# A streaming-encoder layer on one core: row factors of the first block from a natural read, the second block's rows and squares ahead, its accumulators in two own banks

## The chip, the cores and the metric

The kernel runs on one core of one Trainium2 chip. The metric is the device time of one execution in microseconds (us). The kernel before takes 1491.39 us, the median of three runs (1490.81 to 1494.24).

## The reference

One layer over 2048 rows of 1024 channels in float32. `rmsnorm` divides each row by the root of its mean square; this row factor and its place are what the change is about.

```python
def reference(x, p, mix_norm_g, w_in, ...):
    h = x
    for i in range(DEPTH):                      # DEPTH = 1
        hn = rmsnorm(h, mix_norm_g[i])
        proj = hn @ w_in[i]                     # (2048, 3072)
        u, g_ssm, q, k, v, g_attn = jnp.split(proj, SPLITS, axis=-1)
        y_ssm = s5_branch(u, ...)               # diagonal complex state space, GELU, GLU
        y_ssm = y_ssm * jax.nn.silu(g_ssm)
        y_att = stick_breaking_branch(q, k, v, ...) * jax.nn.silu(g_attn)
        h = h + jnp.concatenate([y_ssm, y_att], axis=-1) @ w_out[i]
        ple_gate = jax.nn.sigmoid(rmsnorm(h, ple_norm_g[i]) @ w_ple_gate[i])
        h = h + ple_gate * (p[i] @ w_ple_proj[i])
    return h
```

## The kernel before

The rows are cut into eight blocks of 256 (T0 to T7), each of two halves a and b of 128 rows. Every product of float32 operands is made of three matmuls (`mm3`, L536): each operand is split into a high half (a copy on ScalarE, ACT) and a low half (a subtraction on VectorE, DVE), and high x high, high x low and low x high are added in PSUM.

The first stage, `phase_u` (L546), makes the input of the state-space branch, `ps_u`, in 96 matmuls of 256 columns for each block: four column tiles (`ct`) times eight slices of channels (`c`) times three. T0 comes from a second copy of its rows that the host has turned (channels on partitions); `load_plain` (L552) loads it in pieces between the eight weight tiles and splits both at once, without the row factor. The factor is brought in afterwards: `norms` (L573) squares the turned rows on ACT, in place (L575), adds the eight slices in three steps on GpSimd (POOL, L577), sums over partitions by a matmul with ones (L579), takes the power -1/2 on POOL (L581), puts the factor on a diagonal on DVE (L583) and spreads it by a second matmul (L585) into a `row` tile on ACT (L586). T0's four `ps_u` are then multiplied by `row` on DVE (L633).

T1 to T7 go through `load_x` (L588): the rows are loaded as they lie (L593), squared and summed on ACT (L596), the factor `rs_x` is made by a scaling on DVE (L72) and a power on POOL (L507), the rows are scaled on ACT (L598), turned by 16 transposes of 64 columns on TensorE (PE, L526) into the banks z0 and z1, split from there (`xt<-ps_x`: high halves on ACT L513, low halves on DVE L65), and stored to `hn` (L602) for later stages. Their `ps_u` are copied out on ACT (L635).

Beside this, DVE runs `ssm_chain` (L176) and then `ssm_pack`: the powers and tables of the state-space branch, several hundred small rows on the tiles `ex_`, `sc_`, `pr_`, `pwr`, `pwi`, `cm` and `tabs`. They have no other engine in between.

After `phase_u` come the state-space batches (`ssm_batch`) with the gate products (`ps_sg`) between them, then attention, and the output.

The order on each engine is not that of the code. A planner (`arrange`, L1554) takes all instructions, with what they need of each other, computes a start for each from costs of its own in six turns (`best_order`, L1521; `list_schedule`, L1446), and fixes the order of each engine's instructions by it. Within an engine the instructions run in that order, and one that waits holds up all behind it. Three hints go in: `e.first` (these come ahead of all else), `e.mark(n)` (a place) and `e.later(n)` (DMAs in it are not planned ahead of mark n). All loads of x and all stores of `hn` are on SP's queue, in one order.

[...] `e.bank(name, tags)` takes the next of the tags in turn; before, the accumulators of T0 and of T1 share the banks w0, w1, o and acc, one column tile in each, and T1 can't write them until T0's are multiplied out.

Of the kernel before, what the change touches and what calls it, by code (L numbers as in the profile page):

```python
# [8 lines left out]
F32 = mybir.dt.float32  # L9
F32R = mybir.dt.float32r  # L10
BF16 = mybir.dt.bfloat16
I32 = mybir.dt.int32
AF = mybir.ActivationFunctionType
ALU = mybir.AluOpType
# [4 lines left out]
P = 128  # L19
SEQ = 2048  # L20
DM = 1024
# [17 lines left out]
EPS = 1e-6  # L39
# [24 lines left out]
def vt(nc, out, a, b, op):  # L64
    nc.vector.tensor_tensor(out, a, b, op=op)  # L65


def vs(nc, out, a, s1, op0, s2=None, op1=None):
    if op1 is None:
        nc.vector.tensor_scalar(out, a, s1, None, op0=op0)  # L70
    else:
        nc.vector.tensor_scalar(out, a, s1, s2, op0=op0, op1=op1)  # L72
# [400 lines left out]
def load_w(e, blocks, width, scale, tag="w", pool=None, bufs=None, at=0, act=True, spare=None):  # L473

    nc = e.nc
    out = []
    for c, src in enumerate(blocks, at):
        t = (pool or e.wpool).tile([P, 2, width], F32R, tag=tag, name=f"w_{tag}", **({"bufs": bufs} if bufs else {}))
        hi, lo = t[:, 0], t[:, 1]
        if spare is None or c < STB + STA:  # L480
            raw = e.stage[c % len(e.stage)].tile([P, 512], F32, tag="wst", name="wst")[:, :width]
        else:
            raw = spare.tile([P, L, NCH // 2], F32, tag="uq", name="wst", bufs=4).rearrange("p j c -> p (j c)")[:, :width]
        if c == MARK0 and spare is not None:
            e.mark(0)
        e.wdma(raw.rearrange("p (k c) -> p k c", k=src.shape[1]) if len(src.shape) == 3 and src.shape[0] == P else raw, src)
        if scale is None:
            split(e, hi, lo, raw)
        else:
            if act:  # L490
                nc.scalar.activation(hi, raw, AF.Copy, scale=scale[:, c:c + 1])  # L491
            else:
                vs(nc, hi, raw, scale[:, c:c + 1], ALU.mult)
            stt(nc, lo, raw, scale[:, c:c + 1], hi.bitcast(F32), ALU.mult, ALU.subtract)
        out.append(t)
    return out


def row_blocks(src, n, c0):
    return [src[c * P:(c + 1) * P, c0:c0 + 512] for c in range(n)]  # L500


def rms_rstd(e, pool, ss, n, width, tag):
    nc = e.nc
    r = pool.tile([P, n], F32, tag=f"rs_{tag}", name=f"rs_{tag}")
    vs(nc, r, ss, 1.0 / width, ALU.mult, EPS, ALU.add)
    nc.gpsimd.tensor_tensor(r, r, e.mhalf[:, :n], op=ALU.pow)  # L507
    return r


def split(e, hi, lo, src):

    e.nc.scalar.activation(hi, src, AF.Copy)  # L513
    vt(e.nc, lo, src, hi.bitcast(F32), ALU.subtract)
# [14 lines left out]
def turned(e, name, tags, views):  # L529
    ps, views = turned_into(e, name, tags, views)  # L530
    with e.abreast():
        transposes(e, ps, views)
    return [p[:, :64 * len(views)].rearrange("p (k t) -> p k t", t=64) for p in ps]


def mm3(e, out, ws, xs, first, last):  # L536

    wh, wl = ws
    xh, xl = xs
    mm = e.nc.tensor.matmul  # L540
    mm(out, wh, xh, start=first, stop=False)  # L541
    mm(out, wh, xl, start=False, stop=False)  # L542
    mm(out, wl, xh, start=False, stop=last)  # L543


def phase_u(e, pool, xp, chain):  # L546

    nc = e.nc

    plain = []  # L550

    def load_plain(T):  # L552
        xt = xp.tile([P, 2, 2, NC8, P], F32R, tag="xg", name="xt", bufs=2)
        w = []
        for hf in range(2):
            plain.append(pool.tile([P, NC8, P], F32, tag="x", name="x", bufs=XB))
        for c in range(0, NC8, 2):
            cs = slice(c, c + 2)
            for hf in range(2):
                x = plain[2 * T + hf]  # L560
                nc.sync.dma_start(x[:, cs], e.xt[2 * T + hf, :, cs])
                split(e, xt[:, hf, 0, cs], xt[:, hf, 1, cs], x[:, cs])
            if T == 0:
                w += load_w(e, row_blocks(e.w_in[0], NC8, 0)[cs], 512, e.gmix, act=ACT0, spare=pool, at=c)
        for hf in range(2):
            with e.later(1):
                nc.sync.dma_start(e.hn_d[2 * T + hf], xt[:, hf].rearrange("p s c t -> p (s c t)").bitcast(F32))
        return xt, w

    ones = pool.tile([P, P], F32, tag="ones", name="ones")  # L570
    nc.gpsimd.memset(ones, 1.0)

    def norms(i):  # L573
        x, r = plain[i], e.rs[i]
        nc.scalar.activation(x, x, AF.Square)  # L575
        for n in (4, 2, 1):
            nc.gpsimd.tensor_tensor(x[:, :n], x[:, :n], x[:, n:2 * n], op=ALU.add)  # L577
        ps = e.bank("ps_row", "tr", "ssm")
        nc.tensor.matmul(ps[:, :1], x[:, 0], ones[:, :1], start=True, stop=True)  # L579
        vs(nc, r, ps[:, :1], 1.0 / DM, ALU.mult, EPS, ALU.add)  # L580
        nc.gpsimd.tensor_tensor(r, r, e.mhalf[:, :1], op=ALU.pow)  # L581
        d = pool.tile([P, P], F32, tag="dg", name="dg", bufs=1)
        vs(nc, d, e.ident, r, ALU.mult)  # L583
        ps = e.bank("ps_row", "tr", "ssm")
        nc.tensor.matmul(ps[:, :P], ones, d, start=True, stop=True)  # L585
        nc.scalar.activation(e.row[i // 2][:, i % 2 * P:i % 2 * P + P], ps[:, :P], AF.Copy)  # L586

    def load_x(T):  # L588
        xt = xp.tile([P, 2, 2, NC8, P], F32R, tag="xg", name="xt", bufs=2)
        for hf in range(2):  # L590
            t0 = (2 * T + hf) * P
            x = pool.tile([P, DM], F32, tag="x", name="x", bufs=XB)
            nc.sync.dma_start(x, e.x[0, t0:t0 + P, :])  # L593
            jk = pool.tile([P, DM], BF16, tag="jk", name="jk", bufs=1)
            ss = pool.tile([P, 1], F32, tag="ss", name="ss", bufs=2)
            nc.scalar.activation(jk, x, AF.Square, accum_out=ss)  # L596
            rs = rms_rstd(e, pool, ss, 1, DM, "x")
            nc.scalar.activation(x, x, AF.Copy, scale=rs)  # L598
            for h, ps in enumerate(turned(e, "ps_x", ("z0", "z1"), [x[:, c * P:(c + 1) * P] for c in range(NC8)])):
                d = slice(64 * h, 64 * h + 64)  # L600
                split(e, xt[:, hf, 0, :, d], xt[:, hf, 1, :, d], ps)
            nc.sync.dma_start(e.hn_d[2 * T + hf], xt[:, hf].rearrange("p s c t -> p (s c t)").bitcast(F32))  # L602
        return xt

    xts = {}
    with e.first():
        xts[0], w = load_plain(0)
        norms(0)
        norms(1)
        with e.later(0):  # L610
            xts[1] = load_x(1)
    prep = chain()
    for T in range(NT // 2):
        if 2 <= T + 1 < NT // 2:
            xts[T + 1] = load_x(T + 1)
        xt = xts.pop(T - 2, None)
        xt = xts[T]
        if T % 4 == 0:
            uq = [pool.tile([P, L, NCH // 2], F32, tag="uq", name="uq", bufs=4) for ct in range(4)]
        ps = [e.bank("ps_u", "w0", "w1", "o", "acc", *(("z0", "z1") if T < 1 else ()))[:, :256] for _ in range(4)]  # L620
        if T == 2:
            e.mark(T)
        for ct, c in [(ct, c) for c in range(NC8) for ct in range(4)] if T == 0 else [(ct, c) for ct in range(4) for c in range(NC8)]:
            if T == 0 and ct == 0 and c == MARK1:
                e.mark(1)
            cs = slice(ct * P, (ct + 1) * P)
            mm3(e, ps[ct], (w[c][:, 0, cs], w[c][:, 1, cs]), (xt[:, :, 0, c], xt[:, :, 1, c]), c == 0, c == NC8 - 1)
        n = NCH // 8
        for ct in range(4):
            k0 = (T % 4) * n  # L630
            o, out = ps[ct].rearrange("p (c j) -> p j c", j=L), uq[ct][:, :, k0:k0 + n]
            if T < 1:
                vt(nc, out, o, e.row[T].rearrange("p (c j) -> p j c", j=L), ALU.mult)  # L633
            else:
                nc.scalar.activation(out, o, AF.Copy)  # L635
            if T % 4 == 3:
                c0 = (T // 4) * (NCH // 2)
                nc.gpsimd.dma_start(e.u_d[ct][:, :, c0:c0 + NCH // 2].rearrange("j p c -> p j c"), uq[ct])
    return prep, xts
# [405 lines left out]
def hybrid_block_kernel(ctx: ExitStack, tc: tile.TileContext, x, xt, small, p, w_in, ssm_w_glu, w_out, w_ple_gate,  # L1045
# [115 lines left out]
    up = pool(early, "pu")  # L1161
    e.stage += [pool(early, "stage1", STA)] * STA
    prep, xts = phase_u(e, up, gx, lambda: ssm_chain(e, keep, sm))
    with e.later():
        late_consts()
# [448 lines left out]
```

## Time and profile before

| | |
|---|---|
| median of three runs | 1491.39 us (1490.81 to 1494.24) |
| the profiled execution | 1490.92 us |
| its span, first to last instruction | 1489.2 us |
| mean granted TensorE clock | 0.995 |
| PE, DVE, ACT, POOL busy | 97%, 68%, 55%, 32% of the span |

The profile shows that one execution. Its rows give start and duration in us, the engine, the line, the operation, what it writes and reads, the shapes, how many instructions are merged (x2), and in brackets how long the engine stood idle before and what it waited for. Where rows follow each other without a break, the start of the next one says more than the duration, since rows overlap in the pipeline. The tables of stretches give for each stretch its length, the busy time and count of PE, PEld (weight loads), DVE, ACT and POOL, the granted clock, the share of the DMA engines and GB/s.

### The profile page before, as it was taken

The page shows a single profiled execution, that of the slowest core. Times are in us where ns is not written, and L with a number is a line of the kernel's source. Part 1 is how long each engine was busy: PE and PEld are TensorE (multiplying, and loading weights), DVE is VectorE, ACT ScalarE, POOL GpSimd, SP SyncE. Part 2 cuts the span into 40 slices and gives each one's busy share as a digit, 9 for nine tenths or more (in the row PEclk, how much of TensorE's full clock was granted, in tenths as well). Part 3 has the DMA queues.
Part 4 walks back from the last instruction along what each step waited for, and adds up shares of the span by engine and source line. Part 5 has one row for each costly group of instructions (what it writes and reads, how often), then busy time and mean ns, then how long its engine had stood idle before and what let it go on. Part 6 is the DMA issues. An engine that isn't in the chain of part 4 may idle for free.

```text
span 1489.2 us, 33570 instructions
## 1 busy us (share of the span) xinstructions
PE 1444.9 (97%) x13068; PEld 1220.6 (82%) x13068; DVE 1012.0 (68%) x1814; ACT 812.1 (55%) x1764; POOL 469.2 (32%) x512
## 2 busy tenths in 40 slices
PE   5999999999999999999999999999999999999998
PEld 5999989988888888887788877787777888777776
DVE  8943877976567876777766766657777557744544
ACT  5654545565456765566655655566654436533333
POOL 3221354412221111211122114544234555434332
PEclk9999999999999999999999999999999999999999
DMA  8876746645332523334333445766477546423221
GB/s 292 296 267 231 227 135 206 194 152 169 126 131 99 180 99 101 126 120 141 97 125 126 125 131 183 234 223 187 131 243 243 170 156 196 151 76 107 72 67 60
DMA packets 178909, 238.21 MB, mean 160 GB/s; under 512 B 65744, under 2 KB 121024, under 8 KB 167616
## 3 DMA queue, kind: packets, MB, share of 16 engines
q1 hardware_dynamic: 176368, 227.49, 47.2%
q0 software_dynamic: 2384, 8.59, 2.0%
q8 instruction: 103, 1.69, 0.5%
q14 instruction: 54, 0.44, 0.1%
HBM read 166.94 MB, written 64.90 MB: 156 GB/s over the span
## 4 chain that ended last, share of the span: by engine, by line
PE 77%; DVE 9%; DMA 4%; issue 4%; ACT 3%; POOL 2%; SPq 1%; DVEq 0%; POOLq 0%; ACTq 0%
PE ps_q L745 20%; PE ps_o L843 7%; PE ps_z L812 6%; PE ps_wt L526 4%; PE ps_g L707 4%; PE ps_g L709 4%; PE ps_g L708 3%; PE ps_h L709 3%; PE ps_h L707 3%; PE ps_h L708 3%; DMA wst<-in_ssm_w_glu_dram 2%; PE ps_u L541 1%; PE ps_u L543 1%; PE ps_u L542 1%; PE ps_sg L541 1%
## 5 line engine op out<-in xcount | busy, mean ns | idle before, releaser
L821 DVE TENSOR_TENSOR_SCAN px<-px,ps_z 128x512 f32<-128x512 f32 (+3 forms) x320 | 339.4, 1085 | 102.6 <-ACT px L816 64.5
L745 PE MATMUL ps_q<-w_w,xt 64*128 64x512 f32 x2784 | 372.5, 398 | 1.6 <-DVE old L76 0.9
L745 PEld LDWEIGHTS ps_q<-w_w,xt 64*128 64x128 f32 x2784 | 269.1, 185 | 41.1 <-DVE old L76 1.5
L816 ACT ACTIVATE px<-ps_z 128x512 f32<-128x512 f32 (+3 forms) x320 | 159.5, 534 | 82.5 <-PE ps_z L812 80.8
L835 ACT ACTIVATE ws<-ps_wt 128x512 f32<-128x512 f32 (+3 forms) x320 | 160.3, 537 | 71.8 <-PE ps_wt L526 67.4
L812 PE MATMUL ps_z<-k,q 64*128 64x512 f32 (+3 forms) x960 | 138.0, 381 | 2.1 <-DVE px L821 1.1
L843 PE MATMUL ps_o<-ws,v 128*64 128x128 f32 x2176 | 136.9, 278 | 0.0
L843 PEld LDWEIGHTS ps_o<-ws,v 128*64 128x64 f32 x2176 | 118.6, 138 | 17.0 <-issue 13.7
L507 POOL TENSOR_TENSOR rs_qk<-rs_qk,mhalf 128x4 f32<-128x4 f32 x64 | 67.2, 1050 | 186.5 <-DVE rs_qk L72 183.9
L526 PEld LDWEIGHTS ps_wt<-ident,px 64*128 64x128 f32 x2176 | 94.5, 139 | 29.1 <-ACT ws L835 8.0
L526 PE MATMUL ps_wt<-ident,px 64*128 64x64 f32 x2176 | 100.5, 224 | 5.7 <-ACT ws L835 5.0
L812 PEld LDWEIGHTS ps_z<-k,q 64*128 64x128 f32 x960 | 86.9, 186 | 21.8 <-issue 5.4
L819 POOL TENSOR_SCALAR_AFFINE_SELECT px<-px 128x128 f32<-128x128 f32 x128 | 40.5, 326 | 175.7 <-ACT px L816 167.5
L756 POOL TENSOR_TENSOR v<-qn,v 128x128 f32<-128x128 f32 x64 | 30.9, 483 | 167.6 <-DMA v<-qn 147.8
L541 PE MATMUL ps_u<-xt,w_w 128*128 128x256 f32 x256 | 74.3, 292 | 8.1 <-ACT w_w L491 6.8
L543 PE MATMUL ps_u<-xt,w_w 128*128 128x256 f32 x256 | 73.2, 292 | 2.9 <-DVE w_w L76 2.9
L542 PE MATMUL ps_u<-xt,w_w 128*128 128x256 f32 x256 | 73.8, 289 | 0.5 <-DVE xt L65 0.5
L1026 POOL TENSOR_TENSOR sg<-sg,h 128x512 f32<-128x512 f32 x28 | 39.3, 1412 | 99.7 <-DVE sg L65 90.7
L65 DVE TENSOR_TENSOR yr<-sx,yr 128x512 fp32r<-128x512 f32 x64 | 49.2, 790 | 31.1 <-ACT yr L513 30.2
L65 DVE TENSOR_TENSOR qn<-ps_q,part 128x512 f32<-128x512 f32 x54 | 36.8, 682 | 44.2 <-ACT part L751 40.9
L513 ACT ACTIVATE yr<-sx 128x512 fp32r<-128x512 f32 x64 | 39.3, 629 | 50.2 <-POOL sx L912 17.6
L541 PEld LDWEIGHTS ps_u<-xt,w_w 128*128 128x128 f32 x256 | 50.3, 197 | 8.9 <-ACT w_w L491 7.0
(438 smaller groups left out, 3464.0 us busy)
## 6 DMA issues: line engine op xcount, KB each, us to landing
xt<-hn SPq DMA_DIRECT2D x58, 1024.0 KB
hn<-xt SPq DMA_DIRECT2D x16, 1024.0 KB
h<-h SPq DMA_DIRECT2D x64, 256.0 KB
wst<-in_w_in_dram SPq DMA_DIRECT2D x48, 256.0 KB
xg<-hn SPq DMA_DIRECT2D x12, 1024.0 KB
out_dram<-sg SPq DMA_DIRECT2D x32, 256.0 KB
x<-in_x_dram SPq DMA_DIRECT2D x14, 512.0 KB
h<-in_x_dram SPq DMA_DIRECT2D x28, 256.0 KB
```

Source lines behind the costliest of these rows:

```text
L526: e.nc.tensor.transpose(ps[h][:, 64 * k:64 * k + 64], v[r], e.ident[r, r])
L541: mm(out, wh, xh, start=first, stop=False)
L542: mm(out, wh, xl, start=False, stop=False)
L707: mm(out, xh, wh, start=first, stop=False, skip_group_check=more)
L708: mm(out, xh, wl, start=False, stop=False, skip_group_check=more)
L709: mm(out, xl, wh, start=False, stop=last, skip_group_check=more)
L745: nc.tensor.matmul(o, xt[r, a, c], A.w[c][r, b], start=c + s == 0, stop=c == NC8 - 1 and s == 2)
L812: nc.tensor.matmul(z[:, :n], q[half[h], a], A.k[ch][half[h], b, :n], start=s == 0, stop=s == 2)
L816: nc.scalar.activation(px[:, :n], z[:, :n], AF.Sigmoid, scale=-(HD ** -0.5))
L821: nc.vector.tensor_tensor_scan(rv, rv, z[:, :n][:, ::-1], initial=1.0 if carry[h] is None else carry[h], op0=ALU.mult, op1=ALU.bypass)
L835: nc.scalar.activation(dst, ps, AF.Copy, bias=1.0, scale=-1.0)
L843: nc.tensor.matmul(po[half[h], :P], A.v[sb][:, h], w[:, h, b], start=sb == i, stop=sb == 0)
```

## The change

T0's row factors are made from a second read of the same rows as they lie (`natural`, two tiles of 512 KB out of the weight pool): a load, a square with its sum on ACT, the scaling on DVE and the power on POOL. The six additions on POOL and the two matmuls with one column are gone. T1's loads, squares and factors come ahead of T0's factors in the code, which the planner keeps as a preference. Mark 5 stands at the second natural load; T0's stores of `hn` and the loads of T2 and all later blocks are not planned ahead of it. T1's accumulators lie two by two in the banks tr and ssm (`ps_u1`), which the factors used before; the factors' matmul uses z0 and z1. T0 takes its four banks out of w0, w1, o, acc alone.

```diff
         for hf in range(2):
-            with e.later(1):
+            with e.later(5):
                 nc.sync.dma_start(e.hn_d[2 * T + hf], xt[:, hf]...)
...
+    natural = [e.wpool.tile([P, DM], F32, tag="w", name="xn") for hf in range(2)]
+
     def norms(i):
-        x, r = plain[i], e.rs[i]
-        nc.scalar.activation(x, x, AF.Square)
-        for n in (4, 2, 1):
-            nc.gpsimd.tensor_tensor(x[:, :n], x[:, :n], x[:, n:2 * n], op=ALU.add)
-        ps = e.bank("ps_row", "tr", "ssm")
-        nc.tensor.matmul(ps[:, :1], x[:, 0], ones[:, :1], start=True, stop=True)
-        vs(nc, r, ps[:, :1], 1.0 / DM, ALU.mult, EPS, ALU.add)
+        x, r = natural[i], e.rs[i]
+        if i:
+            e.mark(5)
+        nc.sync.dma_start(x, e.x[0, i * P:(i + 1) * P, :])
+        jk = pool.tile([P, DM], BF16, tag="jk", name="jk", bufs=1)
+        ss = pool.tile([P, 1], F32, tag="ss", name="ss", bufs=2)
+        nc.scalar.activation(jk, x, AF.Square, accum_out=ss)
+        vs(nc, r, ss, 1.0 / DM, ALU.mult, EPS, ALU.add)
         nc.gpsimd.tensor_tensor(r, r, e.mhalf[:, :1], op=ALU.pow)
...
-        ps = e.bank("ps_row", "tr", "ssm")
+        ps = e.bank("ps_row", "z0", "z1")
...
     with e.first():
         xts[0], w = load_plain(0)
+        with e.later(0):
+            xts[1] = load_x(1)
         norms(0)
         norms(1)
-        with e.later(0):
-            xts[1] = load_x(1)
...
         if 2 <= T + 1 < NT // 2:
-            xts[T + 1] = load_x(T + 1)
+            with e.later(5):
+                xts[T + 1] = load_x(T + 1)
...
-        ps = [e.bank("ps_u", "w0", "w1", "o", "acc", *(("z0", "z1") if T < 1 else ()))[:, :256] for _ in range(4)]
+        if T == 1:
+            ps = [b[:, h:h + 256] for b in [e.bank("ps_u1", "tr", "ssm") for _ in range(2)] for h in (0, 256)]
+        else:
+            ps = [e.bank("ps_u", "w0", "w1", "o", "acc")[:, :256] for _ in range(4)]
```

The planner makes a new order from this. On ACT, the stretch from T0's last weight tiles to T1's splits was as follows before (L575 squares T0, L596 squares T1, L598 scales T1, `ps_x` are T1's transposes, a then b):

```order
L575 ACTIVATE x<-x 128x1024
L491 ACTIVATE w_w<-wst,gmix 128x512 x2
L575 ACTIVATE x<-x 128x1024
L596 ACTIVATE jk,ss<-x 128x1024 x2
L598 ACTIVATE x<-x,rs_x 128x1024
L586 ACTIVATE row_179<-ps_row 128x128
L513 ACTIVATE xt<-ps_x_293 128x8x64
L513 ACTIVATE xt<-ps_x_294 128x8x64
L586 ACTIVATE row_179<-ps_row 128x128
L598 ACTIVATE x<-x,rs_x 128x1024
L513 ACTIVATE xt<-ps_x_325 128x8x64
L513 ACTIVATE xt<-ps_x_326 128x8x64
```

The same stretch of the change (L599 squares T1, L601 scales it, L582 squares the natural rows of T0, L589 makes `row`; the last row squares T2a and is followed by both copies of T1's first bank):

```order
L491 ACTIVATE w_w<-wst,gmix 128x512 x2
L599 ACTIVATE jk,ss<-x 128x1024 x2
L601 ACTIVATE x<-x,rs_x 128x1024
L582 ACTIVATE jk,ss<-xn 128x1024
L513 ACTIVATE xt<-ps_x_269 128x8x64
L513 ACTIVATE xt<-ps_x_270 128x8x64
L601 ACTIVATE x<-x,rs_x 128x1024
L582 ACTIVATE jk,ss<-xn 128x1024
L513 ACTIVATE xt<-ps_x_301 128x8x64
L513 ACTIVATE xt<-ps_x_302 128x8x64
L589 ACTIVATE row_179<-ps_row 128x128 x2
L599 ACTIVATE jk,ss<-x 128x1024
```

T0's weights and T1's squares no longer stand behind T0's squares; the natural squares stand between T1's steps.

A little later on ACT, in the stretch of T1's copies (`uq`) and T2's splits, the order before was this (`ps_x_895` is T2a, `ps_x_927` T2b):

```order
L596 ACTIVATE jk,ss<-x 128x1024 x2
L598 ACTIVATE x<-x,rs_x 128x1024
L596 ACTIVATE jk,ss<-x 128x1024
L635 ACTIVATE uq<-ps_u 128x16x16
L598 ACTIVATE x<-x,rs_x 128x1024
L513 ACTIVATE xt<-ps_x_895 128x8x64
L513 ACTIVATE xt<-ps_x_896 128x8x64
L635 ACTIVATE uq<-ps_u 128x16x16
```

In the change (`ps_u_948` and `ps_u_949` are T1's two banks, `ps_x_893` is T2a):

```order
L599 ACTIVATE jk,ss<-x 128x1024
L642 ACTIVATE uq<-ps_u_948 128x16x16 x2
L599 ACTIVATE jk,ss<-x 128x1024
L601 ACTIVATE x<-x,rs_x 128x1024
L599 ACTIVATE jk,ss<-x 128x1024
L601 ACTIVATE x<-x,rs_x 128x1024
L513 ACTIVATE xt<-ps_x_893 128x8x64
L513 ACTIVATE xt<-ps_x_894 128x8x64
```

The first two copies, which need all 48 matmuls of the bank, now stand between the two squares of T2 and ahead of its first scaling.

On DVE, T2b's low halves stood in the middle of the table's 128x128 rows before:

```order
L72 TENSOR_SCALAR rs_x<-ss 128x1
L65 TENSOR_TENSOR pr_t14i<-cm_664,cm_665 128x32
L65 TENSOR_TENSOR cm_672<-tabs,pr_t14r 128x128
L65 TENSOR_TENSOR cm_673<-tabs,pr_t14i 128x128
L65 TENSOR_TENSOR xt<-ps_x_927,xt 128x8x64
L65 TENSOR_TENSOR xt<-ps_x_928,xt 128x8x64
L65 TENSOR_TENSOR cm_674<-tabs,pr_t14i 128x128
L65 TENSOR_TENSOR cm_675<-tabs,pr_t14r 128x128
```

In the change they (`ps_x_925`, `ps_x_926`) stand here:

```order
L65 TENSOR_TENSOR cm_728<-tabs,pr_t22i 128x64
L65 TENSOR_TENSOR cm_729<-tabs,pr_t22r 128x64
L65 TENSOR_TENSOR tabs<-cm_726,cm_727 128x2x32
L65 TENSOR_TENSOR tabs<-cm_728,cm_729 128x2x32
L65 TENSOR_TENSOR xt<-ps_x_925,xt 128x8x64
L65 TENSOR_TENSOR xt<-ps_x_926,xt 128x8x64
L65 TENSOR_TENSOR cm_738<-pr_t22r 128x32
L65 TENSOR_TENSOR cm_739<-pr_t22i 128x32
```

Between the two places lie the rest of the first table (`t14`, `t18`, with its 128x256 rows) and the beginning of the second (`t22`). T3a's split, which stood inside the second table, stands behind it.

## The prediction

> **What bounds the kernel now.** The page comes first. TensorE (PE) is busy nearly the whole span, so what counts is where it is not.
>
> ```profile
> span 1489.2 us, 33570 instructions
> PE 1444.9 (97%) x13068; PEld 1220.6 (82%) x13068; DVE 1012.0 (68%) x1814; ACT 812.1 (55%) x1764; POOL 469.2 (32%) x512
> ```
>
> PE lacks 1489.2 - 1444.9 = 44.3 us. The busy time by stretches (stretch, length, then PE, PEld, DVE, ACT, POOL, clock, DMA) says where:
>
> ```profile
> 0.00:40.00 40.00, 24.61 (x171) 21.82 (x171) 35.24 (x190) 23.60 (x41) 15.16 (x28) 0.91 0.80 290
> 40.00:70.00 30.00, 29.15 (x289) 27.85 (x289) 29.87 (x130) 19.94 (x35) 5.62 (x7) 1.00 0.85 292
> 70.00:140.00 70.00, 69.89 (x651) 68.01 (x652) 32.18 (x49) 32.40 (x64) 14.79 (x13) 1.00 0.79 264
> 140.00:160.00 20.00, 18.37 (x157) 16.59 (x155) 14.52 (x28) 13.47 (x30) 4.54 (x3) 1.00 0.64 190
> 160.00:250.00 90.00, 89.97 (x679) 83.71 (x680) 71.67 (x135) 45.48 (x112) 38.70 (x24) 1.00 0.56 175
> 250.00:350.00 100.00, 95.81 (x895) 89.06 (x895) 83.66 (x141) 59.99 (x139) 38.18 (x34) 1.00 0.59 184
> ```
>
> 15.4 us are lost before 40 us and 0.85 between 40 and 70. From 40 to 70 us VectorE (DVE) is the full engine: 29.87 of 30. It runs the state-space chain (tiles `cm`, `tabs`, `pr_`, `pw`) and, between its rows, the low halves of the split input (`xt<-ps_x,xt`) that PE waits for. So in this stage PE's time is set by **where those splits stand in DVE's queue**. I call the 256-row blocks T0 to T3, their halves a and b.
>
> PE's own rows, in order of time:
>
> ```profile
> 25.57 0.28 PE L543 MATMUL ps_u<-xt,w_w 128*128 128x256 f32 x1
> 33.48 0.58 PE L541 MATMUL ps_u<-xt,w_w 128*128 128x256 f32 x1 [1.17 <-ACT xt L513]
> 34.58 0.58 PE L542 MATMUL ps_u<-xt,w_w 128*128 128x256 f32 x1 [0.52 <-DVE xt L65]
> 35.17 0.41 PE L541 MATMUL ps_u<-xt,w_w 128*128 128x256 f32 x1
> 35.38 0.41 PE L542 MATMUL ps_u<-xt,w_w 128*128 128x256 f32 x1
> 37.85 0.28 PE L543 MATMUL ps_u<-xt,w_w 128*128 128x256 f32 x1
> 37.97 0.28 PE L541 MATMUL ps_u<-xt,w_w 128*128 128x256 f32 x1
> 45.05 0.39 PE L542 MATMUL ps_u<-xt,w_w 128*128 128x256 f32 x1
> ```
>
> T0 ends at 25.85. T1 waits until 33.48 for ACT's high halves and until 34.58 for DVE's low ones. It runs at 0.21 us a matmul (35.17 to 35.38) up to about 37.5, then at 0.12. At 45.05 the transposes of T2b are through and by the built order 32 matmuls of T1 are left: 45.05 + 32 x 0.12 = 48.9, where **T2 starts now**.
>
> **The change, part by part.** *Off DVE's queue.* The additions at L577 leave POOL, and the wait of `rs` for the matmul at L579 goes. DVE's rows beside them are these:
>
> ```profile
> 20.47 1.28 DVE L65 TENSOR_TENSOR pr_den<-pr_t,pr_t 128x32 f32<-128x32 f32 x1
> 21.67 1.88 DVE L76 SCALAR_TENSOR_TENSOR w_w<-wst,gmix,w_w 128x512 fp32r<-128x512 f32 x2
> 24.34 0.16 DVE L72 TENSOR_SCALAR rs<-ps_row 128x1 f32<-128x1 f32 x1 [0.78 <-PE ps_row L579]
> 24.47 0.68 DVE L76 SCALAR_TENSOR_TENSOR sc_h<-sc_w,sc_h 128x32 f32<-128x32 f32 x1
> 25.62 0.77 DVE L72 TENSOR_SCALAR sc_ms<-sc_ms 128x32 f32<-128x32 f32 x1
> 26.82 0.52 DVE L65 TENSOR_TENSOR sc_h<-sc_s,sc_m 128x32 f32<-128x32 f32 x1
> 20.42 4.68 POOL L577 TENSOR_TENSOR x<-x 128x512 f32<-128x512 f32 x4 [14.06 <-ACT x L575]
> 37.82 0.18 DVE L65 TENSOR_TENSOR cm<-pr_cs 128x32 f32<-128x32 f32 x1
> 37.94 0.19 DVE L65 TENSOR_TENSOR pr_t<-pwi,pr_lr 128x32 f32<-128x32 f32 x1
> ```
>
> The wait (0.78) is gone. A 128x32 row takes 0.18 (37.82), and its follower begins 0.12 later; beside POOL's additions `pr_den` took 1.28, `sc_h` 0.68, `sc_ms` 0.77, the second `sc_h` 0.52, and two `w_w` of 128x512 took 1.88, where two `xt` of that width take 1.29 (below). I take all of the excess as relief: 0.78 + 1.10 + 0.50 + 0.59 + 0.34 + 0.59 = **3.9 us**; the other end is 0.8, the wait alone.
>
> *T1.* In the built order T1b's low halves stand behind more chain than before and ahead of the four `uq` products of T0.
>
> ```profile
> 30.79 0.57 DVE L65 TENSOR_TENSOR uq<-ps_u,row 128x256 f32<-128x256 f32 x1
> 33.24 1.29 DVE L65 TENSOR_TENSOR xt<-ps_x,xt 128x512 fp32r<-128x512 f32 x2
> 34.44 0.29 DVE L65 TENSOR_TENSOR cm<-pwi 128x128 f32<-128x128 f32 x1
> ```
>
> They ended at 34.44. Four products of 0.49 go behind them (-2.0), the chain from 34.44 to 37.94 comes ahead less one `rs_x` (+3.4), the relief is -3.9: 31.9. T1 flows from 32.7 instead of 35.1, **2.4 us earlier**; with a cold start of 4 us and T2a's transposes (0.65) it ends near 46.0. The own banks take away the wait for T0's products, which is needed, since these now follow. The natural reads, 512 KB each, stand on SP behind T1's loads and ahead of T0's stores; DVE's queue reaches the two `rs_x` at 23.5 and 26.4 only, and that hides loads and squares: T1's squares began without a wait for a load at 22.42 (row below, with the ACT rows), and even from there the sums would stand at 23.6 and 24.8. Beyond that T1 would move by what the loads are late, T2 not, by what follows.
>
> *T2.* Here DVE's order turns against PE. T2b's low halves stood behind the second of the 128x128 `cm` rows; now they stand behind the whole next table, with its 128x256 rows:
>
> ```profile
> 46.23 1.28 DVE L65 TENSOR_TENSOR xt<-ps_x,xt 128x512 fp32r<-128x512 f32 x2
> 47.43 0.39 DVE L65 TENSOR_TENSOR cm<-tabs,pr_t14i 128x128 f32<-128x128 f32 x1
> 53.73 1.28 DVE L65 TENSOR_TENSOR xt<-ps_x,xt 128x512 fp32r<-128x512 f32 x2
> 54.92 0.21 DVE L65 TENSOR_TENSOR cm<-tabs 128x32 f32<-128x32 f32 x1
> 56.29 0.19 DVE L65 TENSOR_TENSOR cm<-pr_t22r 128x32 f32<-128x32 f32 x1
> 44.41 0.71 PE L526 MATMUL ps_x<-ident,x 64*128 64x64 f32 x16
> ```
>
> What comes ahead of them is 47.43 to 56.29 without T3a's split (53.73 to 54.92): 8.86 - 1.19 = 7.7. They end at 47.4 + 7.7 - 3.9 = 51.2. PE's order then has T3a's 16 transposes (0.65) before T2: **T2 starts at 51.9, 3.0 later**, and PE has only transposes from 46.0 on. The gain of T1 is swallowed whole. T3a's transposes, which came after T2's start, are done: -0.65.
>
> ACT gets a new wait: the copies of T1's first bank stand for its 48th matmul, at about 39.6, with T2b's square and T2a's scale behind them.
>
> ```profile
> 22.42 1.04 ACT L596 ACTIVATE jk<-x 128x1024 bf16<-128x1024 f32 x1
> 23.58 1.06 ACT L596 ACTIVATE jk<-x 128x1024 bf16<-128x1024 f32 x1
> 39.49 0.36 ACT L635 ACTIVATE uq<-ps_u 128x256 f32<-128x256 f32 x1
> ```
>
> 39.6 + 2 x 0.3 + 1.16 gives T2b's sum at 41.4; DVE comes to it at about 43.3. DVE's queue covers that wait by 1.9 us; beyond that it would add to T2's delay one for one.
>
> *The clock.*
>
> ```profile
> 31.00:32.00 1.00, 0.81 (x16) 0.82 (x16) 1.00 (x4) 0.13 (x1) 0.00 (x0) 0.50 0.74 283
> 37.00:38.00 1.00, 1.00 (x9) 1.00 (x8) 1.00 (x7) 0.61 (x1) 0.36 (x1) 0.77 1.01 422
> 65.00:70.00 5.00, 4.15 (x36) 3.78 (x34) 5.00 (x11) 2.66 (x5) 2.19 (x2) 1.00 0.99 325
> ```
>
> After T0's end at 25.85, with little but transposes, the granted clock fell to 0.50 within 5 us and came back about 4 us after T1 began: 4.0/0.215 = 18.6 matmuls at 0.095 more, 1.8 us. T2 will follow 5.9 us of the same kind, so I take **+1.8**; the other end is 0. T1 pays this in both kernels. [...]
>
> *Later.* The 0.85 us that PE lost at 69 us, waiting for another such split, goes: DVE is then ahead and PE later. From 140 to 350 us PE lost 1.63 + 0.03 + 4.19 = 5.9 us. The order is changed there too, up to PE matmul 2936 of 11721, and the same on all engines behind. I can't price it by rows; the ends are -5.9 (all stalls gone) and +5.9 (as much again). I take 0, since the same planner chose both orders.
>
> **Sum:** +3.0 - 0.65 + 1.8 - 0.85 = **+3.3 us**. The profiled execution took 1490.92 us, 1.7 around its span; the median is 0.47 higher. 1491.39 + 3.3 = 1494.7.
>
> **The rivals.** *The state-space stage gains (faster).* DVE's chain ends 3.9 us sooner, and if the stalls between 140 and 350 us hang on that chain, they go: 3.3 - 5.9 = -2.6, 1488.8. It decides if DVE's lead survives until 140 us. Against it: from 70 to 140 us DVE was busy 32.18 of 70, so the lead turns into idle time. For it: gate matmuls are drawn ahead of the first packing, which may cover the 1.63. 17%.
>
> *The relief is not there (slower).* If the slow rows have another cause than POOL's additions, only the 0.8 goes and T2 starts 3.1 later still: +6.4; with 0.7 of the new ACT wait, whose cover is thin, +7.1, 1498.5. For it: the rows show that the two lie side by side, not that one slows the other. Against it: DVE's rows of the same shapes ahead of 20 us have no such length. 15%.
>
> *The clock holds at T2:* +1.5, 1492.9. 10%.
>
> *The change doesn't bring T1 forward.* If T1's loads were late, T1 would start near 33.5 as now, and would still end before 51.2, where DVE releases T2; the sum stays 1494.7, and its chance is within the forecast's.
>
> **How the numbers follow.** Forecast 53%, the rivals 42%, 5% for orders that I misread. A measurement of this kernel tells about 0.3%, 4.5 us, from no change. Slower by more: the relief rival, 13 of the forecast's 53 (stalls added later) and half of the rest, 31%. Faster by more: the tail of the first rival, 7%. Within: 62%. The range goes from the first rival, 1488.8, to the second, 1498.5.
>
> **What would show it.** In the profile after: T0 ending near 23.3 (its last `w_w` splits are freed from POOL's additions), T1's stream near 32.7, DVE full from 4 to 65 us without L577 on POOL, PE idle between about 46 and 52 but for transposes, T2's first matmuls 0.21 apart, no stall near 69, and every matmul from 350 us on shifted by one amount. If T2 starts before 50 us, the queue accounting is wrong; if PE's idle time from 140 to 350 us differs from 5.9 by over 2 us, that stage decides and not the start.

## The result, and the profile after

The changed kernel takes 1510.68 us (median of four runs, 1509.75 to 1512.58), beside 1491.83 for the kernel before on the same chip: 1.0126 times as long, with an interval of 1.0108 to 1.0143. That is 18.9 us more, where 3.3 were predicted, and above the range. The profiled execution took 1511.46 us.

The page of the changed kernel, its span and PE's line:

```profile
span 1509.7 us, 33565 instructions
PE 1451.6 (96%) x13064; PEld 1227.2 (81%) x13064; DVE 1013.0 (67%) x1814; ACT 813.1 (54%) x1766; POOL 458.9 (30%) x506
```

PE lacks 58.1 us where it lacked 44.3: 13.8 more of standing idle. It is also busy 6.7 longer with four matmuls fewer, so some of its work ran slower; the mean granted clock is 0.989, before it was 0.995. The stretches of the changed kernel (columns as before) say where:

```profile
0.00:40.00 40.00, 25.07 (x172) 23.47 (x173) 34.72 (x210) 20.46 (x36) 8.28 (x20) 0.87 0.88 317
40.00:70.00 30.00, 26.60 (x236) 25.42 (x235) 28.23 (x108) 19.66 (x34) 4.76 (x7) 0.89 0.71 267
70.00:140.00 70.00, 67.99 (x639) 66.18 (x639) 26.88 (x44) 34.36 (x65) 15.53 (x15) 1.00 0.73 240
140.00:160.00 20.00, 19.95 (x173) 18.52 (x171) 13.23 (x22) 9.86 (x23) 2.11 (x2) 1.00 0.94 293
160.00:250.00 90.00, 86.79 (x647) 80.78 (x646) 70.48 (x128) 46.17 (x109) 38.26 (x23) 1.00 0.52 164
250.00:350.00 100.00, 89.60 (x761) 84.86 (x759) 82.04 (x132) 55.24 (x125) 34.59 (x29) 0.97 0.52 157
```

The input stage (to 140 us) shows the predicted delay, but the large change is the last row: 10.4 us of idle PE instead of 4.2, 134 matmuls fewer, and a granted clock of 0.97 instead of 1.00.

How the delay grows is seen by marking the same matmuls in both traces. The table gives their start in before, and for the change and for every later run how much later (+) they start in its profiled execution. T1 to T7 are the first `ps_u` matmuls of a block; the last `ps_y` ends the state-space batches, the last `ps_g` is near the end of the kernel.

| run | T1 | T2 | T4 | T7 | last `ps_y` | last `ps_g` | time against before (interval) |
|---|---|---|---|---|---|---|---|
| before, start in us | 33.5 | 49.0 | 76.5 | 116.2 | 311.9 | 1482.7 | 1 |
| the change | -0.6 | +4.6 | +4.6 | +6.7 | +17.8 | +20.7 | 1.0126 (1.0108 to 1.0143) |
| E1 | -0.8 | +4.4 | +4.0 | +6.2 | +6.2 | +8.2 | 1.0039 (1.0025 to 1.0052) |
| E2 | 0.0 | +0.4 | -0.8 | +7.0 | +18.5 | +22.2 | 1.0137 (1.0121 to 1.0153) |
| E3 | -3.7 | -1.6 | -0.1 | -0.1 | +0.2 | +0.2 | 0.9991 (0.9979 to 1.0003) |
| E4 | -1.3 | +4.0 | +4.1 | +7.7 | +18.8 | +20.2 | 1.0134 (1.0116 to 1.0152) |
| E5 | -3.1 | -2.9 | -1.6 | -1.6 | -1.6 | -1.5 | 0.9987 (0.9977 to 0.9996) |
| E6 | +0.3 | +1.6 | +1.5 | +1.5 | +3.9 | +9.8 | 1.0059 (1.0044 to 1.0073) |
| E7 | +0.8 | +2.0 | +5.1 | +5.1 | +13.2 | +22.4 | 1.0161 (1.0140 to 1.0182) |
| E8 | +18.3 | +18.6 | +17.4 | +17.2 | +22.2 | +24.7 | 1.0157 (1.0140 to 1.0175) |
| E9 | +0.3 | +0.4 | +3.4 | +7.0 | +6.9 | +7.5 | 1.0032 (1.0020 to 1.0044) |
| E10 | +0.4 | +4.8 | +5.0 | +4.8 | +9.1 | +11.3 | 1.0076 (1.0058 to 1.0094) |
| E11 | -1.1 | +4.0 | +3.6 | +5.8 | +15.3 | +15.3 | 1.0102 (1.0084 to 1.0121) |
| E12 | -1.2 | +4.0 | +3.2 | +6.8 | +22.4 | +23.3 | 1.0156 (1.0132 to 1.0181) |

For the change, T7 is 6.7 late and the end 20.7: **13.9 us are lost behind T7**, in a stage that the edit doesn't touch, 11.1 of them by the last `ps_y`. The waits of PE in that stage (140 to 350 us; what waited for what, us in total, times, longest), first of before and then of the change:

```profile
PE ps_q L745 <- DVE gsq L65: 1.6, 1, 1.6
PE ps_z L812 <- ACT k L788: 0.9, 1, 0.9
PE ps_y L464 <- DVE rot L65: 0.7, 1, 0.7
```

```profile
PE ps_y L461 <- ACT tp L455: 3.1, 2, 2.3
PE ps_qk L714 <- DVE gsq L65: 2.6, 1, 2.6
PE ps_z L819 <- DVE sg L65: 2.0, 1, 2.0
PE ps_y L461 <- DVE gsq L65: 2.0, 3, 0.9
PE ps_pack L340 <- DVE bn L65: 1.2, 1, 1.2
```

PE now waits longer for the state-space batches themselves: `ps_y` for `tp` 3.1 us and for `gsq` 2.0, `ps_pack` for `bn` 1.2, where in before these are 0.9, 0.3 and 0.2. Three of the longer waits are paid twice, as the stretches around them show (length, PE busy, ..., clock in the third column from the end):

```profile
307.10:310.50 3.40, 1.15 (x9) 1.15 (x10) 2.75 (x6) 3.35 (x7) 1.20 (x1) 1.00 0.32 102
310.50:313.90 3.40, 3.40 (x18) 3.40 (x17) 2.58 (x6) 1.01 (x2) 1.20 (x1) 0.50 0.50 157
331.00:334.40 3.40, 1.47 (x14) 1.32 (x16) 3.07 (x7) 2.27 (x6) 0.54 (x2) 1.00 0.73 209
334.40:337.80 3.40, 3.40 (x26) 3.24 (x24) 0.75 (x1) 0.48 (x2) 0.00 (x0) 0.50 0.69 216
348.00:351.40 3.40, 2.03 (x22) 1.53 (x18) 2.97 (x5) 1.96 (x6) 0.53 (x3) 1.00 0.80 185
351.40:358.20 6.80, 6.69 (x55) 5.19 (x56) 5.15 (x12) 4.02 (x11) 1.71 (x3) 0.50 0.67 268
```

In each of the three, a stretch in which PE did little is followed by one or two stretches of 3.40 us with a granted clock of 0.50. Of PE's busy time, 3.40 + 3.40 + 6.69 = 13.5 us ran at that clock. T1's matmuls of this kernel come 0.21 us apart at 0.50 (34.45 to 37.01) and 0.12 at 1.00 (37.43 to 44.38); by that pace 13.5 x (1 - 0.12 / 0.21) = 5.8 us of work is lost, an estimate, since these are other matmuls. With 7.8 more of idle time in this stage (13.67 instead of 5.85) that is 13.6, against the 13.9 measured.

### The profile page after: what moved, and what is told of

Read it like the earlier page. It is cut to its first block, busy times and chain, and to the rows that moved or that the text cites. A ratio compares the mean times of both kernels' runs of the same rounds, so it can differ in the third digit from the quotient of the medians.

```text
span 1509.7 us, 33565 instructions
## 1 busy us (share of the span) xinstructions
PE 1451.6 (96%) x13064; PEld 1227.2 (81%) x13064; DVE 1013.0 (67%) x1814; ACT 813.1 (54%) x1766; POOL 458.9 (30%) x506
## 3 DMA queue, kind: packets, MB, share of 16 engines
q8 instruction: 103, 1.69, 0.4%
## 4 chain that ended last, share of the span: by engine, by line
PE 77%; DVE 9%; DMA 5%; ACT 3%; issue 3%; POOL 1%; SPq 1%; POOLq 0%; DVEq 0%; ACTq 0%
PE ps_q L752 20%; PE ps_o L850 7%; PE ps_z L819 6%; PE ps_wt L526 4%; PE ps_g L714 4%; PE ps_g L716 4%; PE ps_g L715 3%; PE ps_h L716 3%; PE ps_h L714 3%; PE ps_h L715 3%; DMA wst<-in_ssm_w_glu_dram 2%; PE ps_u L541 1%; PE ps_u L542 1%; PE ps_u L543 1%; DMA v<-qn 1%
## 5 line engine op out<-in xcount | busy, mean ns | idle before, releaser
L541 PE MATMUL ps_u<-xt,w_w 128*128 128x256 f32 x256 | 76.2, 299 | 6.7 <-ACT w_w L491 6.7
L543 PE MATMUL ps_u<-xt,w_w 128*128 128x256 f32 x256 | 74.2, 296 | 1.8 <-DVE w_w L76 1.8
L542 PE MATMUL ps_u<-xt,w_w 128*128 128x256 f32 x256 | 75.5, 296 | 0.0
```

## The experiments

The theory after the result was *order*: the planner's new order of the state-space stage costs the 14 us. Its first rival was *delay*: that stage loses because the input stage hands over 6.7 us later, whatever its order. To tell them apart, an order can be written out: in E1, E2, E3, E5, E11 and E12 the planner's order is replaced by a list of instruction numbers for each engine.

```diff
 def arrange(tc, pools, rows):
     ops, pre, *rest = plan(tc, pools)
-    _, order, _ = best_order(ops, pre, *rest, rows)
+    order = {}
+    for e, v in _PIN.items():
+        b = zlib.decompress(base64.b85decode(v))
+        order[e] = list(struct.unpack(f"<{len(b) // 2}H", b))
```

**E1**, the change with the old order behind the input stage.

> The changed kernel, but every instruction behind the input stage (phase_u) stands on its engine in the order of before; the input stage keeps the order of after. Theory 'order' (the planner's new order of the state-space stage costs the 14 us): 4 to 8 us above before, 1496 to 1500, and PE idle from 140 to 350 us back near 6. Rival 'delay' (that stage loses because the input stage hands over 6.7 us later, whatever its order): 17 us or more above before, 1509 or more, PE idle there near 13.7 as in after.

Measured: 1498.99 us, 1.0039 times before. The table shows T7 6.2 late and the last `ps_y` 6.2 late. E1's stretch from 140 to 350 us, beside that of the change:

```profile
140.00:350.00 210.00, 204.14 (x1698) 189.43 (x1699) 168.46 (x296) 115.08 (x269) 79.68 (x57) 0.99 0.59 182
```

```profile
140.00:350.00 210.00, 196.33 (x1577) 184.17 (x1575) 165.75 (x281) 111.28 (x256) 74.96 (x54) 0.98 0.56 173
```

PE is idle 5.86 us, as in before. Up to the last `ps_y` the late input is passed on one for one. By the last `ps_g` 2.0 us more are lost. E1's granted clock from 250 to 350 us is 0.98, where before's is 1.00; as about 4 us at 0.50 (100 x 0.02 / 0.5) that is 1.7 us by the pace above, an estimate. So *delay* explains at most 2.0 of the 13.9 us and falls as the main cause; *order* stands.

**E2**, the kernel of before with the new order behind its input stage.

> The kernel of before, input stage and its order untouched, but every instruction behind it stands in the order of after. Theory 'order': 10 to 14 us above before, 1501 to 1506. Rival 'delay': within 3 us of before, 1489 to 1494.

Measured: 1513.77 us, 1.0137, more than expected. The merge of the two orders holds up T5 (PE waits 4.58 us at 80.52 for a low half), which isn't the planner's doing. Behind T7 the kernel loses another 22.2 - 7.0 = 15.2 us, though no line of it is changed. So the late order carries its price into a kernel without the edit. As the input is 7.0 late at T7 here too, E2 tells *order* from *delay* only together with E1.

**E3**, the change in the old order throughout.

> The change with the order of before for everything but what the change itself moves: the natural reads behind T1's loads, their squares on ACT behind T1's, the row factors and T0's uq products behind T1's splits, the copies of T1's banks where their last matmul allows. DVE's splits of T2 stand where they stood before. If the late T2 comes from the place of its splits in DVE's queue and the rest from the later order, T1 flows 2 to 3 us earlier than 33.2, T2 no later than 48.7, and the kernel takes 1487 to 1492. If the natural reads or the own banks cost time by themselves, T1 or T2 is late here too and it takes 1495 or more.

Measured: 1492.39 us, 0.9991, no difference from before within the interval, and 0.4 above the expected range. T1 starts 3.7 earlier (2 to 3 were expected), T2 1.6, T4 0.1. The edit itself costs nothing, and its lead on PE is used up by T4. DVE's rows with a wait in E3 suggest why it wasn't ahead:

```profile
23.36 0.15 DVE L72 TENSOR_SCALAR rs<-ss 128x1 f32<-128x1 f32 x1 [0.62 <-ACT jk L582]
24.25 0.29 DVE L70 TENSOR_SCALAR dg<-ident,rs 128x128 f32<-128x128 f32 x1 [0.33 <-POOL rs L584]
29.29 1.29 DVE L65 TENSOR_TENSOR xt<-ps_x,xt 128x512 fp32r<-128x512 f32 x2 [0.91 <-ACT xt L513]
32.61 0.29 DVE L70 TENSOR_SCALAR dg<-ident,rs 128x128 f32<-128x128 f32 x1 [0.69 <-PE ps_row L588]
35.83 0.61 DVE L65 TENSOR_TENSOR uq<-ps_u,row 128x256 f32<-128x256 f32 x1 [1.01 <-ACT row L589]
```

Five waits of together 3.56 us stand against what DVE had gained; E5 tries whether they matter.

**E4**, the planner told the true memory. The planner hands out the slots of the weight pool in the order of first use. By that it has the 7th and 8th gate weight tile follow two `w_in` tiles, that is T7; in the built program these two share memory with the natural reads.

```diff
-                    q = turn[t.tag] = turn.get(t.tag, -1) + 1
+                    r = "xn" if t.name.startswith("xn") else t.tag
+                    q = turn[r] = turn.get(r, 13 if r == "xn" else -1) + 1
```

> The changed kernel as it is, planned anew with one correction in the planner's model of memory: the two natural reads take the slots of the weight pool that they really share with the 7th and 8th gate weight tile, where the planner of after believes that these two tiles wait for T7's last products. Third theory 'wrong slots' (that belief makes the planner's later order bad): 4 to 8 us above before, at most 1502. If the belief does not matter, the order is just another one from the same planner and the time stays within 4 us of 1511.

Measured: 1513.39 us, 1.0134, within the 4 us of "just another order". This theory of mine fell: correcting the belief did not bring the old order back.

**E5**, E3 with DVE's waits filled. In E3's lists `rs`, `dg`, T1b's low halves and the `uq` products move back on DVE, and the row copies on ACT.

> As the third run (the change in the order of before), but on DVE the rows that waited between 23 and 36 us (the two rs rows and dg rows of T0, T1b's low halves, T0's four uq products) stand 0.7 to 2 us further back behind rows of the chain, and on ACT the two row copies stand behind T2's squares. That takes out most of the 3.6 us that DVE idled there. Theory 'DVE's queue bounds the input stage up to 70 us': T2 starts 2 to 3 us before 47.1, T4 2 to 3 us before 76.1, the kernel takes 2 to 3.5 us less than before, 1489 to 1491 beside a before of 1492.5. Rival 'loads, ACT or the clock bound it': T4 stays within 0.5 us of 76.1 and the time within 1 us of before's.

Measured: 1490.58 us (median of twelve runs), 0.9987 (0.9977 to 0.9996). T2 starts 2.9 earlier than in before and T4 1.6, which is 1.2 and 1.4 more than in E3, and the 1.6 stays nearly whole to the end. DVE still waits 1.6 us between 20 and 36 us. Both gains are smaller than the 2 to 3 expected, but T4 did not stay where it was, as the rival had it. Moving rows back on DVE moved T2, T4 and the end, which fits DVE's queue as the bound of the input stage; the two copies on ACT moved with them, so that DVE alone does it is not shown. This is the one version that is faster than before, by 1.9 us by the ratio (0.6 to 3.4 by the interval).

**E6 and E7**, the kernel of before, with the planner stopped early, at five and two orders of its six.

```diff
-    _, order, _ = best_order(ops, pre, *rest, rows)
+    _, order, _ = best_order(ops, pre, *rest, rows, 5)
```

> The kernel of before, nothing changed but that its planner stops after five orders and keeps the fifth, where it made six and kept the sixth. Theory 'the planner's orders of the state-space stage are worth several us either way': the time differs from before by 3 us or more, likely 3 to 8 slower, with the difference arising between 100 and 360 us. Rival, the step of the prediction that took 0 because one planner chose both orders: within 3 us.

> As the run with five orders, with two. Theory 'orders are worth several us': 10 to 30 us above before. Rival: within 3 us.

Measured: 1502.02 us (1.0059) and 1516.74 us (1.0161). E6 is 8.8 us slower by the ratio, just above the 8 that were called likely. Behind T7 they lose 8.3 and 17.3 us; of E6's 8.3, 5.9 come behind the last `ps_y`, so the order of later stages counts too. So the same planner makes orders of the same kernel that differ by as much as the whole effect of the change. Both are orders that the planner itself gave up for a later turn, so they show how far orders lie apart, not what its last choice is worth.

**E8**, the natural reads alone, in the old place of `norms`, with hints and banks of before.

> The kernel of before with one part of the change alone: T0's row factors from natural reads. The rest (T1's loads behind them, banks, hints) as in before, planned anew. Theory 'any replanning moves the late stage': T7 starts 3 to 10 us late because the natural reads stand ahead of T1's, and the stage from 140 to 360 us adds or takes several us of its own: 1497 to 1520 in all. Rival 'only the whole change does it': late stage within 2 us of before's, and the time is what the input stage loses, under 1500.

Measured: 1515.81 us, 1.0157. Here the reads stand ahead of T1's work without the new hints. ACT and PE in E8:

```profile
33.49 1.06 ACT L582 ACTIVATE jk<-xn 128x1024 bf16<-128x1024 f32 x1 [15.52 <-DMA xn<-in_x_dram]
```

```profile
41.53 0.80 PE L588 MATMUL ps_row<-dg,ones 128*128 128x128 f32 x2 [16.56 <-DVE dg L70]
```

ACT stands 15.52 us for the read, to 33.49, and PE 16.56 us for what follows from it, to 41.53: T7 is 17.2 late, where 3 to 10 were expected. The late stage adds 24.7 - 17.2 = 7.5.

**E9 and E10**, the other two parts alone: T1's loads ahead of T0's factors, and T1's own banks, each with the rest of before.

> The kernel of before with one part of the change alone: T1's rows are loaded and squared ahead of T0's row sums (which stay the old ones, by POOL's additions); banks and hints as before, planned anew. T1's flow should come no later than 33.2. Theory 'each new order of the late stage is a new draw': from 140 us to the end the shift against before changes by 3 us or more either way, most likely a loss, since every other order tried lost there: 1494 to 1510. Rival 'only the natural reads or the banks spoil that stage': the shift of T7 passes through unchanged within 2 us.

> The kernel of before with the other part alone: T1's accumulators in two own banks, two blocks of columns in each. T2 within 3 us of 48.7, since DVE's splits release it. Theory 'each new order of the late stage is a new draw': the shift of T7 against before changes by 3 us or more by the end, most likely a loss: 1494 to 1510. Rival: it passes through unchanged within 2 us.

Measured: 1498.62 us (1.0032) and 1504.15 us (1.0076). E10 adds 11.3 - 4.8 = 6.5 behind T7, as the theory had it. Its T2 starts at 53.8, not within 3 us of 48.7: with the banks alone, too, the planner puts T2b's low halves behind the four 128x256 `cm` rows of the table. E9's T1 starts at 33.7, not by 33.2. E9 adds 0.5 behind T7: its new order of the late stage is as good as the old, and there the rival's line was right. A new order is not always a worse one. All the same, of the seven other planned orders (the change, E4, E6 to E10) six cost 6.5 to 17 us behind T7 and none gained. That the natural reads or the banks spoil the stage by themselves is out by E1, which has both and the old order there.

**E11 and E12**, the change with its own order up to 215 us and up to 255 us, and the old order behind.

> The changed kernel; its own order up to its 1606th matmul on PE (about 215 us), the order of before behind that, with as much of a merge between them as the dependences need. It asks where the 14 us of the late stage arise. If behind 215 us: 6 to 9 us above before, 1498 to 1502, like the first run. If ahead of it: 15 us or more above before, 1508 or more.

> As the run before, with the changed kernel's own order up to its 1903rd matmul on PE (about 255 us). If the loss arises in the last stretch, where PE waits at 270 to 350 us, and is made there: 6 to 9 us above before. If it is made between 215 and 255 us, by what is put first there, and only shows behind 270 us: 15 us or more.

Measured: 1507.15 us (1.0102) and 1514.80 us (1.0156), both in the range named for a loss that is made ahead of the seam. They show less than that. E12 loses 23.3 - 6.8 = 16.5 us behind T7, 2.6 more than the change itself, so a seam between two orders can cost time too. In E11 the loss comes at the seam: PE is idle 6.0 us between 215 and 255 us, 3.8 of them in one wait of `ps_tq`, transposes for attention, and the last `ps_y` and `ps_g` are both 15.3 late.

```profile
215.00:255.00 40.00, 33.98 (x233) 29.88 (x232) 22.65 (x42) 15.44 (x37) 14.44 (x11) 0.96 0.37 117
```

Where the change falls behind is better seen beside E1, whose input is nearly as late (T7 6.2 and 6.7) and which loses nothing up to the last `ps_y`. These are the stretches of the change, and then of E1:

```profile
140.00:255.00 115.00, 111.73 (x864) 103.78 (x863) 87.05 (x153) 59.46 (x138) 41.68 (x27) 1.00 0.59 183
255.00:290.00 35.00, 31.33 (x267) 29.33 (x266) 34.39 (x47) 17.33 (x40) 17.70 (x9) 1.00 0.71 228
```

```profile
140.00:255.00 115.00, 113.33 (x874) 105.69 (x873) 88.13 (x165) 59.58 (x143) 42.14 (x26) 1.00 0.59 185
255.00:290.00 35.00, 34.55 (x304) 32.85 (x303) 34.81 (x48) 20.97 (x48) 22.69 (x11) 1.00 0.74 229
```

By 255 us the change is 1.6 us behind E1 on PE, 1.1 on DVE and 0.5 on POOL. From 255 to 290 us it falls back 3.2 more on PE and 5.0 on POOL, while DVE is full in both, 34.4 and 34.8 of 35 us. The matmuls of `ps_y` in the same stretches (busy time and count, clock, DMA) show it too, the change first:

```profile
140.00:255.00 115.00, 19.03 (x155) 1.00 0.59 183
255.00:290.00 35.00, 6.40 (x49) 1.00 0.71 228
```

```profile
140.00:255.00 115.00, 20.20 (x160) 1.00 0.59 185
255.00:290.00 35.00, 10.12 (x80) 1.00 0.74 229
```

Of the gate products (`ps_sg`) PE does nearly as many from 255 to 290 us in both, 146 and 147. So the change's batches fall behind E1's mainly behind 255 us, not because PE is given more gate products there; with DVE full, which of its rows come first may decide. Which moved instructions cost the time, and how much of the loss is already laid ahead of 255 us, as E11 would have it, stays open.

## Why the prediction was wrong

**The step that failed** is *Later*: "I take 0, since the same planner chose both orders", with ends of -5.9 and +5.9. The term measures +13.9. The ends were taken from what PE lost there now (5.9), as if the order could at worst lose as much again. E6 and E7 give the scale that was needed: other orders by the same planner, with nothing changed, cost 8.3 and 17.3 us behind T7. That one planner chose both is no reason for equal worth. The planner's own sums said so: `best_order` works out an end for each turn's order and keeps the earliest. These modelled ends are no chip times; they are 1415.7 us for before and 1425.8 for the change, 10.2 later, of which the input stage was to take 3.3 by the prediction. Why the planner found no better order for the change isn't shown; E4 rules out one reason. The prediction's own test (PE idle differing from 5.9 by over 2 us between 140 and 350) came out at 7.8 and named the right stage.

**The input stage** came out nearly as worked out. Counted from T0, which starts 0.7 later in this execution, the terms are these:

| term | predicted | measured |
|---|---|---|
| T2 starts later | +3.0 | +3.9 |
| T3's transposes done, and the clock of 0.50 at T2 | -0.65 + 1.8 = +1.15 | +1.2 (T3 against T2) |
| the stall at 69 us goes | -0.85 | -1.2 (T4 against T3) |
| sum at T4 | +3.3 | +3.9 |
| T6 | 0 | +2.2 |
| behind T7 | 0 | +13.9 |

*T0, T1 and T2.* PE's rows of the change:

```profile
23.90 0.28 PE L543 MATMUL ps_u<-xt,w_w 128*128 128x256 f32 x1
32.84 0.56 PE L541 MATMUL ps_u<-xt,w_w 128*128 128x256 f32 x1
47.49 0.28 PE L543 MATMUL ps_u<-xt,w_w 128*128 128x256 f32 x1
48.93 0.27 PE L526 MATMUL ps_x<-ident,x 64*128 64x64 f32 x1 [1.16 <-DVE xt L65]
51.92 0.36 PE L526 MATMUL ps_x<-ident,x 64*128 64x64 f32 x1 [1.68 <-DVE xt L65]
53.56 0.58 PE L541 MATMUL ps_u<-xt,w_w 128*128 128x256 f32 x1
57.56 0.41 PE L541 MATMUL ps_u<-xt,w_w 128*128 128x256 f32 x1
```

T0 ends at 24.2 (predicted 23.3, without the 0.7). T1 flows from 32.8 (32.7), and ends at 47.8 instead of 46.0: the prediction's own terms, 32.7 + 4.0 + 77.4 x 0.12 + 0.65, give 46.6, the granted clock of 0.50 held for 4.6 us of T1 (32.84 to 37.43) instead of 4.0, and two matmuls of `ps_row` stand in between for 0.45. Then PE has only transposes until T2 at 53.6 (51.9). T2's matmuls come 0.21 us apart at a granted clock of 0.50 (53 to 57 us; 0.55 from 57 to 58) for 4.0 us and a little more, to 57.56 and beyond, as taken. The wait is the predicted one, T2b's low halves in DVE's queue:

```profile
51.18 1.28 DVE L65 TENSOR_TENSOR xt<-ps_x,xt 128x512 fp32r<-128x512 f32 x2
```

They end at 52.4, 1.2 after the forecast (51.2), 0.7 of it the later start. E3 and E5, with the splits in their old place, have T2 early.

*The relief on DVE.* The slow rows are gone in the change:

```profile
22.57 0.18 DVE L65 TENSOR_TENSOR pr_den<-pr_t,pr_t 128x32 f32<-128x32 f32 x1
22.67 0.18 DVE L76 SCALAR_TENSOR_TENSOR sc_h<-sc_w,sc_h 128x32 f32<-128x32 f32 x1
22.77 0.18 DVE L70 TENSOR_SCALAR sc_ms<-sc_ms 128x32 f32<-128x32 f32 x1
```

E9, which keeps POOL's additions, keeps the slow row too; its DVE row, and POOL's beside it:

```profile
20.77 1.29 DVE L65 TENSOR_TENSOR pr_den<-pr_t,pr_t 128x32 f32<-128x32 f32 x1
```

```profile
20.73 4.70 POOL L577 TENSOR_TENSOR x<-x 128x512 f32<-128x512 f32 x4 [14.37 <-ACT x L575]
```

So the rival "the relief is not there" falls: `pr_den` took 1.29 us instead of 0.18 beside additions of 4.70 / 4 = 1.2 each. How the additions hold the row up isn't shown.

*ACT's new wait.* Its cover at T2 held. But the same kind of wait, which the prediction looked for at T1 alone, struck at T6: copies of T5's banks stand ahead of T6's high halves and wait for T5's matmuls. ACT's rows, then PE's:

```profile
98.13 0.38 ACT L642 ACTIVATE uq<-ps_u 128x256 f32<-128x256 f32 x1 [2.90 <-PE ps_u L543]
101.01 0.38 ACT L642 ACTIVATE uq<-ps_u 128x256 f32<-128x256 f32 x1 [2.49 <-PE ps_u L543]
101.29 1.08 ACT L513 ACTIVATE xt<-ps_x 128x512 fp32r<-128x512 f32 x2
```

```profile
102.66 0.27 PE L526 MATMUL ps_x<-ident,x 64*128 64x64 f32 x1 [1.69 <-DVE xt L65]
```

That wait of 1.69 is most of the 2.2 at T6. It sits in the order of the input stage: E1, which keeps that order, shows it too (T7 6.2 late, T4 4.0).

*The rivals.* "The state-space stage gains" looked at the right stage with the wrong sign: DVE's lead was idle time by 140 us, as the prediction feared. "The clock holds at T2" did not happen: 0.50 was granted there from 53 to 57 us.

## What to carry to other kernels

Where a planner lays out the instructions, an edit is also a new order of the stages that it doesn't touch. Price that by how far the planner's orders of the unchanged kernel lie apart (8 and 17 us here), not by what the stage loses now. Writing the old order out for the untouched stages tells edit and order apart in one run.

The planner's modelled ends would have warned. They are 1415.7 us for before, 1416.7 for E9, 1418.5 for E6, 1423.6 for E10, 1425.8 for the change, 1428.2 for E4, 1432.5 for E7 and 1434.0 for E8, and rank the kernels as the chip does, but for the last two.

A lead on a busy engine can be lost again in waits of that engine (3.56 us in E3). And a kernel that comes late must be compared with one that comes as late: beside before, the change has done 6.5 us less on POOL by 255 us, beside E1 only 0.5.

## What was not expected of the hardware

The granted clock fell without a stretch of full idleness. The rows above have PE busy for 1.15 and 1.47 of 3.40 us, with no single wait over 2.3, and the next 3.40 us at 0.50. Yet this stretch of the change, with 1.49 us, is followed by a clock of 1.00:

```profile
880.50:883.90 3.40, 1.49 (x26) 1.24 (x24) 0.00 (x0) 0.70 (x2) 0.67 (x2) 1.00 0.46 105
883.90:887.30 3.40, 1.95 (x21) 1.41 (x23) 2.96 (x4) 3.40 (x7) 0.00 (x0) 1.00 0.97 213
```

And 2.03 us at 348.0 was followed by 0.50. So busy time alone doesn't decide it here, since 1.49 us kept the clock and 2.03 us lost it; what else counts stays open. All stretches at 0.50 in the traces of before and of the change are multiples of 3.41 us in length, by the traces' clock records, but for those cut off by the end: 3.41 at 310.5 in the change, 6.83 around T1 in before, 10.24 there in the change. Why they have these lengths isn't shown.
